# A two-layer MLP kernel: operand blocks of the second layer copied to PSUM ahead of the subtraction that makes their low half

## The chip, the core and the metric

One core of a Trainium2 chip runs the whole program. The metric is device time of one execution in microseconds; the kernel before has a median of 1340.35 us over 3 runs (1339.38 to 1341.3). The engines go by these names: TensorE (PE in the profile, with PEld for its weight loads), VectorE (DVE), ScalarE (ACT), GpSimd (POOL) and SyncE (SP), which issues the DMAs.

## What is computed

A layer of a trunk: a gated DeltaNet mixer with a residual, then a squared-ReLU MLP with a residual, each behind an RMS norm, and a final RMS norm. 1024 tokens, width 1024, 4096 hidden channels, all fp32. Cut to the part that matters here:

```python
def sq_relu_mlp(h, w1, w2):
    return jnp.square(jax.nn.relu(h @ w1)) @ w2

def reference(x, ...):
    h = x
    h = h + gated_deltanet(rmsnorm(h, norm_mix_g[0]), ...)
    h = h + sq_relu_mlp(rmsnorm(h, norm_mlp_g[0]), mlp_w1[0], mlp_w2[0])
    return rmsnorm(h, final_norm_g)
```

## The kernel before

The program has four stages, one after the other: the mixer (to about 554 us), its output projection and the second norm (to 642), the first MLP layer (to 973) and the second (973 to 1324), with the final norm woven into the end of the last.

**Split operands.** TensorE multiplies in the fp32r format. To keep fp32's accuracy each operand is split into a high part (the value rounded to fp32r) and a low part (the value less the high part, again as fp32r), and a product is three matmuls: high by high, high by low, low by high (L1284, L1285, L1286 in the second layer; L1285 is the one that needs the low part of the moving operand, L1286 that of the stationary one). `split` (L79) does this: with "act" ScalarE casts the source to the high part (L81), then VectorE subtracts the high part from the source (L86).

**The second layer** is the product of the squared hidden channels (A) and w2 (B). The 32 tiles of hidden channels are cut into five groups, numbered 0 to 4, of 2, 2, 4, 4 and 4 channel tiles in each half (`GROUPS`). In a group A and B are cut in two both ways, and the four blocks of the result come of seven products P1 to P7 (Winograd's form of Strassen's method), so the operands are the blocks A11, A12, A22, B11, B21, B22 and the block sums S1 to S4 (of A) and T1 to T4 (of B). The loop `for q, (n, k, p, x, y) in enumerate(seq)` runs over the 35 products: n is the group, k the place in the group, p the product's number, x and y its operands. The order of a group is P1, P2, P5, P7, P6, P4, P3; in the last group P1, P5, P7, P6, P4, P2, P3. A product has four blocks of 128 tokens (m), each in a PSUM bank of its own, from four banks in turn; for each m there are 2 or 4 steps of three matmuls 128x128 by 128x512, so a product is 24 matmuls in groups 0 and 1 and 48 in the others.

**Operands.** A block lies in SBUF in one or two units of 128x1024 fp32 (two channel tiles by 512 columns), the tiles `u`. They are loaded by DMA from w2 and from the spilled hidden channels (`hd`), or made by `make_sum` (L918), on GpSimd but for T1 and T3, which VectorE makes; a sum mostly takes the place of one of its operands. `make_operand` (L928) splits a block, unit by unit, into a slot of `hT` (two slots for either side): while product q runs, the operands of product q+1 go into the slots that product q-1 used, so the cast waits for TensorE to have read those. 7 x (2 + 2 + 4 + 4 + 4) = 112 units are split so.

**After each block m** the bank is added on VectorE (L1214) to the running sum of its product, in `oT` (P2, P3, P4, P7) or the tiles P1, P5, P6 (`extra`); in group 0 the sums in `extra` begin with a ScalarE copy (L1302). In the last group `finish_up` combines the seven sums (more adds L1214 on VectorE and GpSimd, with both operands in SBUF), then come the squares of the final norm on ScalarE (L1221), its roots on GpSimd (L1225, L76) and the rows of y on VectorE (L1239).

**What sets the order.** The code is written in program order with `next(pieces)` after each m, and a scheduler orders the instructions of each engine; each engine then runs its own queue strictly in order, waiting on semaphores. [...] 

Of the kernel before, what the change touches and what calls it, by code (L numbers as in the profile page):

```python
# [8 lines left out]
F32 = mybir.dt.float32  # L9
F32R = mybir.dt.float32r  # L10
AF = mybir.ActivationFunctionType
ALU = mybir.AluOpType

P = 128
T = 1024          # tokens
D = 1024          # model width
KT = D // P       # contraction tiles of the model width
NT = T // P       # token tiles, also chunks of the recurrence
H = 8             # heads
# [3 lines left out]
NW = 8            # buffers of half a weight tile, split  # L23
NRAW = 2          # buffers of half a weight tile, as loaded
NKK = 12          # key-side buffers
# [3 lines left out]
def trunk_kernel(  # L29
# [18 lines left out]
    ps = ctx.enter_context(tc.tile_pool(name="ps", bufs=1, space=bass.MemoryType.PSUM))  # L48
    dram = ctx.enter_context(tc.tile_pool(name="dram", bufs=1, space=bass.MemoryType.DRAM))

    def ps_gemm(name):
        """Two banks, one for each half of the columns."""
        return [ps.tile([P, 512], F32, tag="gemm", name=f"{name}_{i}", bufs=4) for i in range(2)]

    def ps_tp(name):
        return ps.tile([P, 512], F32, tag="tp", name=name, bufs=2)

    # ---------------------------------------------------------------- constants
# [6 lines left out]
    pvec = const.tile([P, 105], F32, tag="pvec", name="pvec")       # conv taps, g_o, g_mix  # L65
# [6 lines left out]
    def rsqrt_pool(dst, src, n, add=EPS):  # L72
        """dst = (src + add) ** -0.5 on [P, n]."""
# [4 lines left out]
    # -------------------------------------------------- weights, split exactly  # L78
# [14 lines left out]
    def load_split(hi, lo, src, name, eng):  # L93
        """Load half a weight tile and split it."""
        split(hi, lo, load_raw(hi, src, name), eng)

    def load_wtile(w, c0, name, eng):
        """Columns c0..c0+127 of w as [k, kt, 128], in two halves of kt; eng: None for the loads alone."""
# [10 lines left out]
    def load_wrow(src, name, eng, pool, tags):  # L109
        """128 rows of w as [k, D]."""  # L110
# [6 lines left out]
    def gemm_T(pt, w, act, half, during=None):  # L117
        """pt[half] = w_tile^T @ act for half the tokens, act given as [k, 2, kt, T]; during: what to emit before which step."""
# [10 lines left out]
    def norm_to_T(src, t, g_bc, dstT, pool, hs, name):  # L129
        """RMS norm of token tile src [P, D], times g, transposed into dstT [k, 2, kt, T]."""  # L130
# [23 lines left out]
    # ------------------------------------------------------ norm, gates, decays  # L154
# [3 lines left out]
    def small(shape, parts=P):  # L158
        """Room for a small array."""
# [8 lines left out]
    # per-channel vectors, from rows to columns  # L168
# [19 lines left out]
    tpv = ps.tile([P, 512], F32, tag="ch", name="tpv", bufs=2)  # L188
    nc.tensor.transpose(tpv[:, 0:105], pv, ident[0:105, 0:105])
    # taps and g_o are halved: silu(x) = (tanh(x / 2) + 1) * x / 2  # L190
    # (g_o is negated, as the heads' outputs are)
# [5 lines left out]
    def norm_x(t, sq, sc):  # L197
        """Token tile t over its root mean square."""
# [14 lines left out]
    def turn_x(g, tags):  # L213
        """Four token tiles, times g_mix, into xT."""
        tps = [ps.tile([P, 512], F32, tag=tag, name=f"tpx_{g}_{kt}", bufs=4 if tag == "gemm" else 2)
# [23 lines left out]
    # the small projections: high and low parts of the weights side by side  # L239
# [7 lines left out]
    def decays():  # L247
        tab = ps.tile([P, 512], F32, tag="ch", name="tab", bufs=2)
# [9 lines left out]
        # softplus(t) = max(t, 0) + log1p(e), e = exp(-|t|);  # L258
        # log1p(e) = ln(u) + (e - (u - 1)) / u, u = 1 + e rounded
# [14 lines left out]
        # g = -exp(a_log) * softplus(a + dt_bias), as [token, head, tile]  # L274
# [3 lines left out]
        # cumulative sums within a chunk, counted from the middle of the chunk  # L278
# [11 lines left out]
        pg = ps.tile([P, 512], F32, tag="ch", name="pg", bufs=2)  # L290
# [5 lines left out]
        # ne = -exp(G), G from the start of the chunk  # L296
# [1047 lines left out]
```

## Time and profile before

| | |
|---|---|
| median of 3 runs | 1340.35 us |
| span of the profiled execution, first to last instruction | 1335.6 us |
| what lies around the span, median less span | 4.75 us |
| PE busy | 1267.3 us, 95% |
| DVE busy | 1013.7 us, 76% |
| ACT busy | 619.1 us, 46% |
| POOL busy | 410.9 us, 31% |
| second layer, first to last matmul | 972.95 to 1323.95 us |
| the costliest group of instructions: L86 of `hT` on DVE | 204.6 us |

The profile is of one execution; its own time is the span and what lies around it, and the profile gives the span alone. A busy share is an average over the four stages. Matmuls are pipelined, so a busy TensorE isn't TensorE at its full pace: the pace is read from the number of matmuls in a stretch, and the granted clock is given beside it.

### The profile page before, as it was taken

The page shows a single profiled execution, that of the slowest core. Times are in us where ns is not written, and L with a number is a line of the kernel's source. Part 1 is how long each engine was busy: PE and PEld are TensorE (multiplying, and loading weights), DVE is VectorE, ACT ScalarE, POOL GpSimd, SP SyncE. Part 2 cuts the span into 40 slices and gives each one's busy share as a digit, 9 for nine tenths or more (in the row PEclk, how much of TensorE's full clock was granted, in tenths as well). Part 3 has the DMA queues.
Part 4 walks back from the last instruction along what each step waited for, and adds up shares of the span by engine and source line. Part 5 has one row for each costly group of instructions (what it writes and reads, how often), then busy time and mean ns, then how long its engine had stood idle before and what let it go on. Part 6 is the DMA issues. An engine that isn't in the chain of part 4 may idle for free.

```text
span 1335.6 us, 18642 instructions
## 1 busy us (share of the span) xinstructions
PE 1267.3 (95%) x6668; PEld 1034.4 (77%) x6668; DVE 1013.7 (76%) x1745; ACT 619.1 (46%) x1458; POOL 410.9 (31%) x339
## 2 busy tenths in 40 slices
PE   7999999999999999999969999999999899899986
PEld 5788888888888887788747888888876678687765
DVE  6799599589759867544796555555579988989998
ACT  4671655554654466333345554555554323333223
POOL 6220122211121112101463233323143615354565
PEclk9999999999999999999979999999999989999988
DMA  5242212122221212311313333333152134142003
GB/s 177 81 108 60 55 49 67 50 60 56 61 75 38 67 40 77 113 48 48 134 47 103 113 109 110 111 115 107 48 220 95 63 100 152 36 138 79 0 1 126
DMA packets 101871, 111.48 MB, mean 83 GB/s; under 512 B 23401, under 2 KB 73746, under 8 KB 101778
## 3 DMA queue, kind: packets, MB, share of 16 engines
q1 hardware_dynamic: 101778, 110.28, 27.0%
q8 instruction: 53, 0.87, 0.3%
q14 instruction: 40, 0.33, 0.1%
HBM read 89.26 MB, written 21.00 MB: 83 GB/s over the span
## 4 chain that ended last, share of the span: by engine, by line
PE 76%; DVE 13%; issue 5%; POOL 3%; ACT 2%; DMA 1%; POOLq 0%; DVEq 0%; ACTq 0%; SPq 0%
PE p L1066 7%; PE p L1065 7%; PE p L1064 7%; DVE hT L86 6%; PE p L1285 5%; PE p L1286 4%; PE p L1284 4%; PE pv L127 2%; PE pv L125 2%; PE pv L126 2%; PE pq L127 2%; PE pq L125 2%; PE pq L126 2%; PE pg L127 2%; PE pg L126 2%
## 5 line engine op out<-in xcount | busy, mean ns | idle before, releaser
L86 DVE TENSOR_TENSOR hT<-u,hT 128x1024 fp32r<-128x1024 f32 x112 | 204.6, 1845 | 20.4 <-ACT hT L81 20.3
L81 ACT CAST hT<-u 128x1024 fp32r<-128x1024 f32 x112 | 111.3, 1049 | 210.6 <-PE p L1285 144.0
L1285 PE MATMUL p<-hT 128*128 128x512 f32 x448 | 180.6, 403 | 22.1 <-DVE hT L86 21.7
L918 POOL TENSOR_TENSOR u<-u,u 128x1024 f32<-128x1024 f32 x48 | 139.1, 2904 | 170.4 <-DVE hT L86 124.8
L1284 PE MATMUL p<-hT 128*128 128x512 f32 x448 | 178.7, 399 | 7.2 <-DVE oT L1214 6.0
L1286 PE MATMUL p<-hT 128*128 128x512 f32 x448 | 178.2, 398 | 0.0
L76 POOL TENSOR_TENSOR sso<-sso,cons 128x1 f32<-128x1 f32 x64 | 42.0, 657 | 266.2 <-DVE sso L611 266.1
L1285 PEld LDWEIGHTS p<-hT 128*128 128x128 f32 x448 | 86.5, 193 | 45.8 <-DVE hT L86 28.2
L1284 PEld LDWEIGHTS p<-hT 128*128 128x128 f32 x448 | 86.4, 193 | 29.8 <-DVE oT L1214 5.6
L1286 PEld LDWEIGHTS p<-hT 128*128 128x128 f32 x448 | 86.7, 194 | 17.8
L1088 DVE TENSOR_TENSOR u<-u,p 128x512 f32<-128x512 f32 x56 | 38.4, 685 | 42.1 <-PE p L1066 42.1
L125 PE MATMUL pg<-xT,wh_g 128*128 128x512 f32 x128 | 54.4, 425 | 0.0
L125 PE MATMUL pq<-xT,wh_q 128*128 128x512 f32 x128 | 53.9, 421 | 0.0
L1214 DVE TENSOR_TENSOR oT<-oT,p 128x512 f32<-128x512 f32 x80 | 52.8, 675 | 1.5 <-PE p L1286 1.5
L125 PE MATMUL pv<-xT,wh_v 128*128 128x512 f32 x128 | 53.6, 419 | 0.0
L125 PE MATMUL pk<-xT,wh_k 128*128 128x512 f32 x128 | 53.1, 414 | 0.0
L127 PE MATMUL pg<-xT,wl_g 128*128 128x512 f32 x128 | 52.4, 409 | 0.0
L1064 PE MATMUL p<-T,wh_S 128*128 128x512 f32 x120 | 48.1, 401 | 4.4 <-ACT T L81 3.5
L127 PE MATMUL pv<-xT,wl_v 128*128 128x512 f32 x128 | 51.7, 404 | 0.0
L126 PE MATMUL pg<-xT,wh_g 128*128 128x512 f32 x128 | 51.7, 404 | 0.0
L126 PE MATMUL pv<-xT,wh_v 128*128 128x512 f32 x128 | 51.5, 402 | 0.0
L126 PE MATMUL pk<-xT,wh_k 128*128 128x512 f32 x128 | 51.1, 399 | 0.0
(312 smaller groups left out, 3470.0 us busy)
## 6 DMA issues: line engine op xcount, KB each, us to landing
u<-in_mlp_w_dram SPq DMA_DIRECT2D x34, 512.0 KB, 3.5
ra<-in_mlp_w_dram SPq DMA_DIRECT2D x28, 512.0 KB, 4.3
u<-hd SPq DMA_DIRECT2D x28, 512.0 KB, 5.7
hd<-u SPq DMA_DIRECT2D x24, 256.0 KB, 3.3
xt<-in_x_dram SPq DMA_DIRECT2D x8, 512.0 KB, 5.2
wr_k<-in_gdn_w_in_dram SPq DMA_DIRECT2D x16, 256.0 KB, 3.2
wr_q<-in_gdn_w_in_dram SPq DMA_DIRECT2D x16, 256.0 KB, 3.0
wr_v<-in_gdn_w_in_dram SPq DMA_DIRECT2D x16, 256.0 KB, 2.9
```

The costliest lines, as they stand in the source:

```text
L81: nc.scalar.copy(h_ap, src)
L86: (nc.gpsimd if low == "pool" else nc.vector).tensor_tensor(out=l_ap, in0=src, in1=h_ap.bitcast(F32), op=SUB)
L125: nc.tensor.matmul(o, hi, act[:, 0, kt, s], start=(kt == 0), stop=False)
L126: nc.tensor.matmul(o, hi, act[:, 1, kt, s], start=False, stop=False)
L127: nc.tensor.matmul(o, lo, act[:, 0, kt, s], start=False, stop=(kt == KT - 1))
L918: (V if name in ("T1", "T3") else G).tensor_tensor(out=o, in0=a, in1=b, op=op)
L1064: nc.tensor.matmul(o, hi[:, kt, :], act(0, kt), start=(j == 0 and kt == 0), stop=False)
L1065: nc.tensor.matmul(o, hi[:, kt, :], act(1, kt), start=False, stop=False)
L1066: nc.tensor.matmul(o, lo[:, kt, :], act(0, kt), start=False, stop=(j == n - 1 and kt == 3))
L1284: nc.tensor.matmul(o, hid(0, kt)[:, s], w(0, kt), start=(kt == 0), stop=False)
L1285: nc.tensor.matmul(o, hid(0, kt)[:, s], w(1, kt), start=False, stop=False)
L1286: nc.tensor.matmul(o, hid(1, kt)[:, s], w(0, kt), start=False, stop=(kt == g - 1))
```

## The change

In the second layer `make_operand` no longer calls `split`. ScalarE casts a unit to the high part as before, and copies the unit as it is into two PSUM banks (`cp`); VectorE subtracts the high part from that copy, so its first operand lies in PSUM instead of SBUF. There are two such buffers of two banks each, in the banks of `tp` and `ch`, which the mixer has left by then; to that end these two go into a pool of their own, closed after the mixer. The squares of the final norm write their discarded output into one of the `cp` buffers. The rest of the program is as it was; the diff also takes out comments and docstrings, which shifts the line numbers. In the changed kernel the cast is L944, the copy L945, the subtraction L946, the block sums L923, the adds L1226, the squares L1233 and the rows of y L1251.

```diff
+    psx = tc.tile_pool(name="psx", bufs=1, space=bass.MemoryType.PSUM)
+    px = psx.__enter__()
...
     def ps_tp(name):
-        return ps.tile([P, 512], F32, tag="tp", name=name, bufs=2)
+        return px.tile([P, 512], F32, tag="tp", name=name, bufs=2)
...
     gdn.__exit__(None, None, None)
+    psx.__exit__(None, None, None)
+    psc = tc.tile_pool(name="psc", bufs=1, space=bass.MemoryType.PSUM)
+    pc = psc.__enter__()
...
         for u, t in enumerate(us):
             hi, lo = (hT[:, hl, 4 * side + 2 * u : 4 * side + 2 * u + 2, HALF[s]] for hl in range(2))
-            split(hi, lo, t, "act")
+            cp = two_banks(f"cp{n}_{name}_{u}")
+            nc.scalar.copy(hi, t)
+            nc.scalar.copy(cp, t)
+            V.tensor_tensor(out=lo, in0=cp, in1=hi.bitcast(F32), op=SUB)
             if u == len(us) - 1:
...
+    def two_banks(name):
+        return pc.tile([P, 2, 512], F32, tag="cp", name=name, bufs=2)
...
-        nc.scalar.activation(ps_tp(f"sq{t}_{n}"), oT[:, t, HALF[n]], AF.Square, scale=1.0 / 32, accum_out=sss[t][:, n : n + 1])
+        nc.scalar.activation(two_banks(f"sq{t}_{n}")[:, 0, :], oT[:, t, HALF[n]], AF.Square, scale=1.0 / 32, accum_out=sss[t][:, n : n + 1])
```

The scheduler sets the new instructions into the queues. In the lines below a name such as `cp3_S1_0` is the copy of unit 0 of operand S1 in group 3, `u18` a unit in SBUF, `p2_0_2_1` the bank of group 0, product P2, block m = 1, and the last number of a name counts tiles.

ScalarE's queue in group 3 before, the casts of S1 and T1 (two units each) and the first of the next operands:

```order
L81 CAST hT_5905<-u18_9220 128x2x512
L81 CAST hT_5905<-u9_9211 128x2x512
L81 CAST hT_5905<-u19_9221 128x2x512
L81 CAST hT_5905<-u0_6640 128x2x512
L81 CAST hT_5905<-u2_6642 128x2x512
```

and now:

```order
L945 COPY cp3_S1_0_10479<-u18_9231 128x1024
L945 COPY cp3_S1_1_10497<-u19_9232 128x1024
L944 CAST hT_5908<-u18_9231 128x2x512
L944 CAST hT_5908<-u9_9222 128x2x512
L944 CAST hT_5908<-u19_9232 128x2x512
L945 COPY cp3_T1_0_10515<-u9_9222 128x1024
L944 CAST hT_5908<-u0_6647 128x2x512
L945 COPY cp3_T1_1_10533<-u0_6647 128x1024
L945 COPY cp3_S3_0_10557<-u2_6649 128x1024
```

The copies of S1's two units come ahead of its casts, those of T1's among the casts.

VectorE's queue at the start of the second layer before: the low parts of B21 and A12 (the second product's operands), the sums T1 and T3, and the first adds of P2 with the low parts of S1 and T1 beside them:

```order
L86 TENSOR_TENSOR hT_5905<-u6_6646,hT_5905 128x2x512
L1088 TENSOR_TENSOR u2_15_9110<-u2_15_9110,p1_15_3_9190 128x512
L86 TENSOR_TENSOR hT_5905<-u1_6641,hT_5905 128x2x512
L918 TENSOR_TENSOR u17_9219<-u5_6645,u4_6644 128x1024
L918 TENSOR_TENSOR u5_6645<-u7_6647,u5_6645 128x1024
L86 TENSOR_TENSOR hT_5905<-u16_9218,hT_5905 128x2x512
L1214 TENSOR_TENSOR oT_84<-oT_84,p2_0_2_0_9277 128x512
L86 TENSOR_TENSOR hT_5905<-u17_9219,hT_5905 128x2x512
```

and now:

```order
L1100 TENSOR_TENSOR u2_15_9117<-u2_15_9117,p1_15_3_9201 128x512
L946 TENSOR_TENSOR hT_5908<-cp0_A12_0_9257,hT_5908 128x2x512
L923 TENSOR_TENSOR u17_9230<-u5_6652,u4_6651 128x1024
L946 TENSOR_TENSOR hT_5908<-cp0_B21_0_9269,hT_5908 128x2x512
L923 TENSOR_TENSOR u5_6652<-u7_6654,u5_6652 128x1024
L1226 TENSOR_TENSOR oT_87<-oT_87,p2_0_2_0_9292 128x512
L946 TENSOR_TENSOR hT_5908<-cp0_S1_0_9299,hT_5908 128x2x512
L1226 TENSOR_TENSOR oT_87<-oT_87,p2_0_2_1_9304 128x512
L946 TENSOR_TENSOR hT_5908<-cp0_T1_0_9311,hT_5908 128x2x512
```

The order of A12 and B21 has changed, and the sum T1 (L923 of u17) stands between them.

ScalarE's queue at the end of the last group before, the last casts (S4 and B22 of the last product) and the squares of the final norm:

```order
L81 CAST hT_5905<-u11_9213 128x2x512
L81 CAST hT_5905<-u6_6646 128x2x512
L81 CAST hT_5905<-u7_6647 128x2x512
L81 CAST hT_5905<-u1_6641 128x2x512
L1221 ACTIVATE sq0_0_11119,ssf0_11118<-oT_84 128x512
L1221 ACTIVATE sq4_0_11122,ssf4_11121<-oT_84 128x512
L1221 ACTIVATE sq4_1_11124,ssf4_11121<-oT_84 128x512
L1221 ACTIVATE sq1_0_11146,ssf1_11145<-oT_84 128x512
L1221 ACTIVATE sq5_0_11149,ssf5_11148<-oT_84 128x512
L1221 ACTIVATE sq5_1_11151,ssf5_11148<-oT_84 128x512
```

and now:

```order
L944 CAST hT_5908<-u6_6653 128x2x512
L944 CAST hT_5908<-u7_6654 128x2x512
L944 CAST hT_5908<-u1_6648 128x2x512
L1233 ACTIVATE sq0_0_11344,ssf0_11343<-oT_87 128x512
L1233 ACTIVATE sq4_0_11347,ssf4_11346<-oT_87 128x512
L1233 ACTIVATE sq4_1_11349,ssf4_11346<-oT_87 128x512
L945 COPY cp4_S4_1_11366<-u7_6654 128x1024
L1233 ACTIVATE sq1_0_11373,ssf1_11372<-oT_87 128x512
L1233 ACTIVATE sq5_0_11376,ssf5_11375<-oT_87 128x512
L1233 ACTIVATE sq5_1_11378,ssf5_11375<-oT_87 128x512
L945 COPY cp4_B22_0_11395<-u6_6653 128x1024
L1233 ACTIVATE sq2_0_11402,ssf2_11401<-oT_87 128x512
```

Three of the four copies of the last product stand between the squares. On VectorE the matching piece, from the add of P2's second block on, is now:

```order
L1226 TENSOR_TENSOR oT_87<-oT_87,p2_4_2_1_11353 128x512
L946 TENSOR_TENSOR hT_5908<-cp4_S4_1_11366,hT_5908 128x2x512
L1226 TENSOR_TENSOR oT_87<-oT_87,p2_4_2_2_11382 128x512
L1251 SCALAR_TENSOR_TENSOR y4_0_11411<-oT_87,ssf4_11346,gx3_0_9236 128x512
L946 TENSOR_TENSOR hT_5908<-cp4_B22_0_11395,hT_5908 128x2x512
L1251 SCALAR_TENSOR_TENSOR y4_1_11414<-oT_87,ssf4_11346,gx3_1_9237 128x512
L1226 TENSOR_TENSOR oT_87<-oT_87,p2_4_2_3_11417 128x512
L1251 SCALAR_TENSOR_TENSOR y5_0_11446<-oT_87,ssf5_11375,gx3_0_9236 128x512
L946 TENSOR_TENSOR hT_5908<-cp4_B22_1_11430,hT_5908 128x2x512
L1251 SCALAR_TENSOR_TENSOR y5_1_11449<-oT_87,ssf5_11375,gx3_1_9237 128x512
```

where before the four low parts of the last product stood ahead of the second add and of all rows of y.

## Rows read from the trace of the kernel before

**Rows 1.** Busy time of each engine by stage: five groups, a clear stretch, the end

```profile
core 0: us, PE busy (x) PEld busy (x) DVE busy (x) ACT busy (x) POOL busy (x), PEclk, DMA share, GB/s
972.95:1018.14 45.19, 41.55 (x169) 31.98 (x168) 41.63 (x33) 23.32 (x31) 23.32 (x9) 0.96 0.57 209
1018.14:1067.70 49.56, 41.74 (x168) 32.24 (x169) 47.85 (x46) 17.72 (x18) 25.16 (x10) 0.97 0.19 64
1067.70:1151.01 83.31, 79.25 (x336) 64.86 (x337) 72.40 (x62) 24.94 (x27) 33.73 (x12) 0.96 0.31 101
1151.01:1232.93 81.92, 77.05 (x337) 62.83 (x336) 73.02 (x61) 27.36 (x29) 36.12 (x13) 1.00 0.32 103
1232.93:1323.95 91.02, 82.08 (x337) 65.48 (x335) 89.72 (x79) 31.19 (x51) 54.16 (x34) 0.94 0.05 19
1083.72:1138.12 54.40, 54.40 (x241) 45.05 (x240) 46.59 (x38) 19.66 (x21) 26.64 (x10) 1.00 0.41 136
1323.95:1335.60 11.65, 0.14 (x1) 0.00 (x0) 7.30 (x10) 2.17 (x5) 6.05 (x7) 0.69 0.58 218
```

**Rows 2.** Who waited for whom: total us, times, longest us

```profile
PE p L1285 <- DVE hT L86: 21.7, 12, 2.4
...
POOL u L918 <- DVE hT L86: 124.8, 26, 17.1
```

**Rows 3.** TensorE's timeline after one wait: start, us, instruction, [idle before]

```profile
1021.05 0.79 PE L1285 MATMUL p<-hT 128*128 128x512 f32 x1 [2.43 <-DVE hT L86]
...
1022.06 0.63 PE L1284 MATMUL p<-hT 128*128 128x512 f32 x1
1022.49 0.63 PE L1285 MATMUL p<-hT 128*128 128x512 f32 x1
```

**Rows 4.** VectorE's subtractions and adds: ns least/median/most; then busy us, mean ns

```profile
L86 DVE TENSOR_TENSOR hT<-u,hT x112: 1208/1225/3412, 956.6 to 1313.0; 128x1024 fp32r<-128x1024 f32 x112
...
L145 DVE TENSOR_TENSOR hT<-tpn_h,hT x16: 678/680/692, 572.0 to 648.9; 128x512 fp32r<-128x512 f32 x16
...
L1214 DVE TENSOR_TENSOR oT<-oT,p x80: 671/674/687, 983.9 to 1328.2; 128x512 f32<-128x512 f32 x80
...
L1214 DVE TENSOR_TENSOR oT<-oT,P x12: 677/922/2510, 1267.5 to 1308.4; 128x512 f32<-128x512 f32 x12
...
L86 DVE TENSOR_TENSOR hT<-u,hT 128x1024 fp32r<-128x1024 f32 x112 | 204.6, 1845 | 20.4 <-ACT hT L81 20.3
```

**Rows 5.** Block sums: GpSimd's durations; then VectorE's and GpSimd's timeline in group 2

```profile
L918 POOL TENSOR_TENSOR u<-u,u x48: 2354/3258/3392, 976.2 to 1275.5; 128x1024 f32<-128x1024 f32 x48
...
1138.62 3.43 DVE L918 TENSOR_TENSOR u<-u,u 128x1024 f32<-128x1024 f32 x1
1141.97 0.67 DVE L1214 TENSOR_TENSOR oT<-oT,p 128x512 f32<-128x512 f32 x1
1142.57 1.21 DVE L918 TENSOR_TENSOR u<-u,u 128x1024 f32<-128x1024 f32 x1
1143.71 0.67 DVE L1214 TENSOR_TENSOR oT<-oT,p 128x512 f32<-128x512 f32 x1
...
1135.22 5.75 POOL L918 TENSOR_TENSOR u<-u,u 128x1024 f32<-128x1024 f32 x2 [1.16 <-DVE hT L86]
```

**Rows 6.** ScalarE's casts and squares: ns least/median/most; then its timeline

```profile
L81 ACT CAST hT<-u x112: 1037/1048/1071, 955.5 to 1303.4; 128x1024 fp32r<-128x1024 f32 x112
L81 ACT CAST wh_A<-ra x42: 603/624/624, 698.1 to 959.3; 128x512 fp32r<-128x512 f32 x42
...
L1221 ACT ACTIVATE sq<-oT x16: 579/580/604, 1311.9 to 1328.9; 128x512 f32<-128x512 f32 x16
...
1149.62 3.89 ACT L81 CAST hT<-u 128x1024 fp32r<-128x1024 f32 x4 [8.99 <-PE p L1285]
```

**Rows 7.** The start of the second layer: timelines of VectorE and GpSimd

```profile
976.07 4.57 DVE L918 TENSOR_TENSOR u<-u,u 128x1024 f32<-128x1024 f32 x2 [0.23 <-ACT u L1084]
...
976.17 10.04 POOL L918 TENSOR_TENSOR u<-u,u 128x1024 f32<-128x1024 f32 x3 [22.05 <-ACT u L1084]
```

More of the change, by code (lines that the diff above doesn't have):

```diff
@@ L187, in trunk_kernel @@
     nc.sync.dma_start(nea, a_log.partition_broadcast(P))
-    tpv = ps.tile([P, 512], F32, tag="ch", name="tpv", bufs=2)
+    tpv = px.tile([P, 512], F32, tag="ch", name="tpv", bufs=2)
     nc.tensor.transpose(tpv[:, 0:105], pv, ident[0:105, 0:105])
@@ L213, in turn_x @@
     def turn_x(g, tags):
-        tps = [ps.tile([P, 512], F32, tag=tag, name=f"tpx_{g}_{kt}", bufs=4 if tag == "gemm" else 2)
+        tps = [(ps if tag == "gemm" else px).tile([P, 512], F32, tag=tag, name=f"tpx_{g}_{kt}", bufs=4 if tag == "gemm" else 2)
                for kt, tag in enumerate(tags)]
@@ L247, in decays @@
     def decays():
-        tab = ps.tile([P, 512], F32, tag="ch", name="tab", bufs=2)
+        tab = px.tile([P, 512], F32, tag="ch", name="tab", bufs=2)
         for t in range(NT):
@@ L289, in decays @@
         nc.vector.memset(hi[64:128, :], 1.0)
-        pg = ps.tile([P, 512], F32, tag="ch", name="pg", bufs=2)
+        pg = px.tile([P, 512], F32, tag="ch", name="pg", bufs=2)
         gv = gg.rearrange("p h t -> p (h t)")
@@ L308, in decays @@
         nc.scalar.activation(cd, cd, AF.Exp)
-        tg = ps.tile([P, 512], F32, tag="ch", name="tg", bufs=2)
+        tg = px.tile([P, 512], F32, tag="ch", name="tg", bufs=2)
         nc.tensor.transpose(tg[0:64, 0:P], gs[:, 0], ident)
@@ L567, in scan @@
         for c in range(NT):
-            ch = ps.tile([P, 4, P], F32, tag="ch", name=f"ch{h}_{c}", bufs=2)
+            ch = px.tile([P, 4, P], F32, tag="ch", name=f"ch{h}_{c}", bufs=2)
             po = ch[:, 3, :]
@@ L1314, in trunk_kernel @@
     hold.__exit__(None, None, None)
+    psc.__exit__(None, None, None)
 _INS = [
```

## Prediction

> **What bounds the kernel now.** I read the busy times by stage first, then what TensorE waits for, then how long one instruction takes alone and in company. The change touches only the second layer, which runs from 973 to 1324 us of the 1335.6 us span, so the share of busy time over the whole kernel says little. In the one stretch of it without a wait, TensorE does five products of 48 matmuls in 54.40 us [rows 1], that is 10.88 us for a product, and half of it, 5.44 us, in groups 0 and 1, whose products have 24 matmuls. Seven products are then 38.1 us in groups 0 and 1 and 76.2 us in groups 2, 3 and 4. The five stages take 45.2, 49.6, 83.3, 81.9 and 91.0 us [rows 1], so they lose 7.1, 11.5, 7.1, 5.8 and 14.8 us, together **46.3 us**. That is all that a change in this layer can give while the matmuls stay the same, apart from the 11.65 us after the last matmul [rows 1]. Of the 46.3, some 29.3 us are idle TensorE (stage less busy time, summed) and some 12 us are half clock: the granted clock of the five stages is 0.96, 0.97, 0.96, 1.00 and 0.94, and stage times (1 - clock) sums to 12.1 [rows 1]. The rest is lost in gaps of a matmul or two.
>
> Who makes TensorE wait? In the second layer it is above all VectorE's subtraction, L86: 21.7 us in 12 waits [rows 2]. [...]
>
> Why is VectorE late? The subtraction of 128x1024 takes 1.225 us as a rule, but its longest is 3.412 us and its mean 1.845 us [rows 4]. What stretches it stands beside it: GpSimd's block sums L918, which take 2.354 us at best, 3.258 us in the middle [rows 5]. Two VectorE sums of the same form show it within 4 us: 3.43 us at 1138.62, beside a GpSimd pair that runs 1135.22 to 1140.97, and 1.21 us at 1142.57, when GpSimd is idle [rows 5]. VectorE's adds with one operand in PSUM don't show it: 80 of them lie between 671 and 687 ns, in the same stages, while the form with both operands in SBUF spreads from 677 to 2510 ns [rows 4]. Summed over the stages VectorE is busy 325 of 351 us, and 89.7 of 91.0 in group 4, ScalarE 125 us [rows 1].
>
> **The change part by part.** *The subtraction from PSUM.* The nearest row is L145, the same subtraction with its first operand in PSUM and fp32r output, at half the size: 680 ns, against 671 to 687 for the adds [rows 4]. An SBUF form goes from 0.677 us at 512 columns to 1.225 at 1024 [rows 4], so I take 1.22 us for 1024 out of PSUM, with bounds of 1.21 (the shortest now) and 1.36 (twice 680 ns). 112 times (1.845 - 1.22) is **70 us less VectorE**. From start to start such an instruction takes 0.07 us less than its duration, 1.14 us, and an add 0.60 [rows 5].
>
> [...] The rows show no difference between the two sources at 512 columns. [...]
>
> *The copy on ScalarE.* Before, no ScalarE copy from SBUF to PSUM of 1024 columns stands in the trace. The cast, SBUF to SBUF, takes 1.048 us at 1024 columns and four in a row take 3.89 us, 0.97 apiece; an activation of 512 columns into PSUM takes 0.58 us [rows 6]. Bounds: 1.0 (0.58 and 0.42 for 512 columns more, which is what lies between the cast's 0.624 and 1.048 [rows 6]) and 1.16 (twice 0.58). I take 1.0 us, 112 us more ScalarE, 125 + 112 = 237 of 351. In a product of 10.88 us that is four casts and four copies, 7.9 us; in group 1 3.9 of 5.44 us; in group 0 three of seven products have four copies of sums into P too, L1302, some 0.5 us each by the 512-column row, 2.0 us more, so 5.9 of 5.44 there, but 33 of 38.1 us over the group. It fits, but barely in group 0.
>
> *Where the copy stands in the queue.* In the steady products the order sets the first two copies ahead of the casts, which wait for TensorE to leave the slot; before, ScalarE stood idle there, 8.99 us ahead of one set of four casts [rows 6]. From the slot's release, about 1.4 us before a product begins, ScalarE then has four casts and two copies, 5.9 us, and VectorE 1.2 us: all is there some 6 us into a product of 10.88. Four to five us of slack, with subtractions that no longer grow to 3.4 us. I cost it at nothing in groups 2 and 3; the slack is its cover.
>
> *Two buffers for the copies.* A third copy waits for the subtraction of the first. In the steady order a cast lies between, and the subtraction (1.2) fits beside two casts (1.9): nothing.
>
> *The operand is free earlier.* L918 overwrites operand blocks and waits 125 us for L86 in all [rows 2]; it will wait for ScalarE's cast and copy instead, and runs nearer to its 2.35 us. GpSimd is busy 23 to 54 us of a stage [rows 1], so that costs and gives nothing by itself. SP's loads into freed blocks go out earlier too, some in another order; the DMA share of the last four stages is 0.05 to 0.32 [rows 1], nothing.
>
> *The start of group 0.* Here the change adds a wait. The second product needs B21's low part. ScalarE's copy of it stands behind the last square of the first layer, for which GpSimd's S1 sum waits too, and that begins at 976.17 now [rows 7]; with the copy of A12 ahead of that square it ends near 977.6. VectorE, in order, does A12's subtraction (to 977.3) and the T1 sum ahead of B21's; the pair T1, T3 took 4.57 us beside GpSimd's sums [rows 7]. T1 alone, 1.2 to 2.9 us, will end at 978.5 to 980.2 and the subtraction 1.2 us later, whereas the second product begins at 978.4 (972.95 and 5.44) and wants it at its second matmul. A stall of 1 to 3 us, and half clock after it. Of its 7.1 us I leave group 0 with 5.5: a gain of 1.6.
>
> *Group 1.* VectorE has 14 subtractions (14 x 1.14 = 16.0), 28 adds at a pitch of 0.6 (16.8) and three SBUF sums at 1.2 to 3.4 (3.6 to 10): 36 to 43 of 38.1 us. It is still nearly the bound: I leave 3 of 11.5, a gain of 8.5.
>
> *Groups 2 and 3.* 28 x 1.14 + 28 x 0.6 and four SBUF sums (5 to 14) are 54 to 63 of 76.2 us. One us left of each: gains 6.1 and 4.8.
>
> *Group 4.* Its VectorE work has 16 SBUF adds more (677 ns to 2510, middle 922 [rows 4]), all in four products: with 16 subtractions and 16 adds, 18.2 + 9.6 + 14.8 = 42.6 of 43.5 us. Balanced. And in the last-but-one product the squares of L1221 now come ahead of the last three copies: B22's second copy stands behind nine squares, the last three of which wait for the third add, 8.2 + 0.7 us into the product; at 0.6 each they end 10.8 us in, the copy 11.8, and its subtraction, behind the fourth add and a row of y, 13.4 to 13.8 us in. The last product begins at 10.88 and wants it seven matmuls later, at 12.5: a stall of about 1 us. I leave 5 of 14.8: a gain of 9.8.
>
> *After the last matmul.* In the 11.65 us there VectorE is busy 7.30 [rows 1], with adds and rows of y that had queued; with less queued this may shrink by 1 or 2. Zero in the sum.
>
> The sum is 1.6 + 8.5 + 6.1 + 4.8 + 9.8 = **30.8 us**. Against the profile, 1335.6 becomes 1304.8; what lies around the span is 4.75 us to the median of 1340.35, so **1309.5 us**.
>
> **The rivals.** *ScalarE's line eats part of it.* If in the 14 products of 5.44 us and in group 4 each set of low parts comes one copy (1.0 us) late, with a half clock here and there, some 14 us go back: about 1324. For it speaks that 5.9 of 5.44 us stand in ScalarE's queue in three products, against it the idle time in rows 6. *All stalls go*, also at the start and in group 4: a gain of 40 to the whole 46.3, 1294 to 1300. For it speaks that only VectorE's 16 L918 and 16 late adds then have both operands in SBUF; the order at the start speaks against it. *The subtraction is stretched as before*, since it still reads its high part from SBUF and writes there: then VectorE stays at 1.845 us, and each of 12 waits is up to a copy longer, 1340 to 1352. The 80 adds of rows 4 read and write SBUF just so and were never stretched. *Slower: the copy into two banks is the bound.* The layer's ScalarE work without copies is 125 us; with 112 copies of c us it fills the 351 us of now at c = 2.0. If a two-bank copy took 2.1 us, it would be 360 us, 1350. The point is twice my 1.0, and rows 6 show 0.58 for half of it, so this needs a cost that no row hints at. *It doesn't do what it says*: the order shows each of the 112 copies and subtractions, so no chance is set aside.
>
> **How the numbers follow.** Forecast, 1300 to 1316 around 1309.5: 0.64. ScalarE eats part, 1316 to 1332: 0.19. All stalls go, 1294 to 1300: 0.08. Stretched as before: 0.05, of which 0.04 within 0.2% of the median (2.7 us, about what a measurement of this kernel can tell) and 0.01 slower. The copy as the bound, slower: 0.04. So faster 0.91, same 0.04, slower 0.05. The range is 1295 to 1327: it leaves out some 0.05 of the second case, 0.01 of the third and the last two, below 0.2 together.
>
> **What would show it.** L86's place: 112 subtractions from cp near 1.22 us with little spread, whatever GpSimd does; ScalarE's copies near 1.0 us; the wait of TensorE for the subtraction falling from 21.7 us to some 6, left at the second product of group 0 and the last of group 4; stages 2 and 3 near 77 us; granted clock 1.00 in groups 2 and 3. It is wrong if the subtractions spread as before, if copies take well over 1.0 us, or if TensorE's waits move to ScalarE's casts or copies.

## The result and the profile after

The changed kernel takes **1294.32 us** (median of 4 runs, 1293.30 to 1295.62) against 1339.87 for the kernel before (4 runs beside it, 1338.58 to 1341.30): a ratio of **0.966**, with a 95% interval of 0.965 to 0.968, or 45.5 us less. The forecast of 1309.5 had the direction and the place of the gain and was 15 us short of its size; the time lies 0.7 us below the low end of the range.

Here are the stages of the second layer after the change, the five groups and what follows the last matmul (stretch, its length, then the busy time of each engine, the granted clock, the DMA share and the GB/s):

```profile
core 0: us, PE busy (x) PEld busy (x) DVE busy (x) ACT busy (x) POOL busy (x), PEclk, DMA share, GB/s
972.19:1014.24 42.05, 40.65 (x169) 32.36 (x168) 31.33 (x31) 35.95 (x45) 23.77 (x9) 0.96 0.62 229
1014.24:1053.27 39.03, 38.45 (x168) 31.61 (x169) 36.53 (x46) 30.67 (x32) 21.16 (x10) 1.00 0.23 78
1053.27:1129.59 76.32, 76.32 (x338) 62.99 (x336) 64.28 (x66) 53.16 (x55) 32.05 (x13) 1.00 0.35 118
1129.59:1205.75 76.16, 76.16 (x338) 63.06 (x336) 59.45 (x61) 54.13 (x57) 31.27 (x12) 1.00 0.31 104
1205.75:1282.73 76.98, 76.47 (x337) 62.79 (x335) 68.97 (x81) 55.66 (x77) 48.75 (x35) 1.00 0.08 31
1282.73:1292.10 9.37, 0.15 (x1) 0.00 (x0) 5.00 (x7) 1.97 (x5) 3.90 (x5) 0.62 0.52 198
```

Read it beside [rows 1]. At the full pace the groups take 38.1, 38.1, 76.2, 76.2 and 76.2 us. They lost 7.1, 11.5, 7.1, 5.8 and 14.8 us before; they lose 4.0, 0.95, 0.15, 0 and 0.8 now, and the end shrank from 11.65 to 9.37. TensorE is the bound of this layer almost everywhere, with a granted clock of 1.00 in groups 1 to 4 and 0.96 in group 0. VectorE's work went from 324.6 us in the five groups to 260.6, ScalarE's from 124.5 to 229.6.

| stage | before | after | gain | gain forecast |
|---|---|---|---|---|
| group 0 | 45.19 | 42.05 | 3.1 | 1.6 |
| group 1 | 49.56 | 39.03 | 10.5 | 8.5 |
| group 2 | 83.31 | 76.32 | 7.0 | 6.1 |
| group 3 | 81.92 | 76.16 | 5.8 | 4.8 |
| group 4 | 91.02 | 76.98 | 14.0 | 9.8 |
| after the last matmul | 11.65 | 9.37 | 2.3 | 0 |
| ahead of the layer | 972.95 | 972.19 | 0.8 | 0 |
| span | 1335.6 | 1292.1 | 43.5 | 30.8 |

The durations of one instruction after the change (least/median/most in ns, then the times of the first and the last start): the subtraction L946 for two of the four kinds of block, ScalarE's copy into two PSUM banks L945, and the block sums L923 on both engines:

```profile
L946 DVE TENSOR_TENSOR hT<-cp_S,hT x32: 1208/1224/1226, 983.2 to 1267.7; 128x1024 fp32r<-128x1024 f32 x32
L946 DVE TENSOR_TENSOR hT<-cp_B,hT x24: 1207/1216/1225, 961.2 to 1273.8; 128x1024 fp32r<-128x1024 f32 x24
...
L945 ACT COPY cp_S<-u x32: 1000/1017/1044, 979.4 to 1266.6; 128x1024 f32<-128x1024 f32 x32
...
L923 POOL TENSOR_TENSOR u<-u,u x48: 2390/2422/3388, 975.8 to 1238.6; 128x1024 f32<-128x1024 f32 x48
L923 DVE TENSOR_TENSOR u<-u,u x16: 1215/1968/3420, 976.3 to 1200.5; 128x1024 f32<-128x1024 f32 x16
```

The longest subtraction takes 1.226 us, where it took up to 3.412 before [rows 4]. GpSimd's sums fell too, in the middle from 3.258 [rows 5] to 2.422 us: each engine had stretched the other. VectorE's own 16 sums, which still read both operands from SBUF, are stretched up to 3.42 us still, and more of them than before, when their middle was 1.216:

```profile
L918 DVE TENSOR_TENSOR u<-u,u x16: 1209/1216/3427, 976.1 to 1227.4; 128x1024 f32<-128x1024 f32 x16
```

What TensorE still waits for on VectorE's subtraction, in the whole layer (us in total, times, longest):

```profile
PE p L1297 <- DVE hT L946: 2.5, 3, 1.4
```

Before it was 21.7 us in 12 waits [rows 2]. The longest of the three is at the second product of group 0, as forecast.

### The profile page after: what moved, and what is told of

Same layout as the page of the kernel before. It is cut to its first block, busy times and chain, and to the rows that moved or that the text cites. A ratio compares the mean times of both kernels' runs of the same rounds, so it can differ in the third digit from the quotient of the medians.

```text
span 1292.1 us, 18789 instructions
## 1 busy us (share of the span) xinstructions
PE 1254.9 (97%) x6668; PEld 1031.8 (80%) x6668; DVE 946.5 (73%) x1745; ACT 725.7 (56%) x1570; POOL 390.8 (30%) x339
## 5 line engine op out<-in xcount | busy, mean ns | idle before, releaser
L1297 PE MATMUL p<-hT 128*128 128x512 f32 x448 | 175.6, 392 | 2.5 <-DVE hT L946 2.5
L1298 PE MATMUL p<-hT 128*128 128x512 f32 x448 | 175.1, 391 | 0.0
L1296 PE MATMUL p<-hT 128*128 128x512 f32 x448 | 174.1, 391 | 0.0
L923 POOL TENSOR_TENSOR u<-u,u 128x1024 f32<-128x1024 f32 x48 | 123.1, 2585 | 150.2 <-ACT cp_T L945 45.1
L944 ACT CAST hT<-u 128x1024 fp32r<-128x1024 f32 x112 | 112.6, 1050 | 30.7 <-PE p L1297 28.9
L1297 PEld LDWEIGHTS p<-hT 128*128 128x128 f32 x448 | 84.6, 189 | 21.7 <-DVE hT L946 3.8
L1296 PEld LDWEIGHTS p<-hT 128*128 128x128 f32 x448 | 84.2, 188 | 18.7 <-ACT P L1314 0.6
L1298 PEld LDWEIGHTS p<-hT 128*128 128x128 f32 x448 | 84.6, 189 | 17.2
L1226 DVE TENSOR_TENSOR oT<-oT,p 128x512 f32<-128x512 f32 x80 | 53.1, 678 | 12.9 <-PE p L1298 12.9
L127 PE MATMUL pg<-xT,wh_g 128*128 128x512 f32 x128 | 54.4, 425 | 0.0
L127 PE MATMUL pk<-xT,wh_k 128*128 128x512 f32 x128 | 53.1, 415 | 0.0
L1078 PE MATMUL p<-T,wl_S 128*128 128x512 f32 x120 | 48.3, 403 | 3.0 <-DVE wl_S L88 3.0
L946 DVE TENSOR_TENSOR hT<-cp_S,hT 128x1024 fp32r<-128x1024 f32 x32 | 39.1, 1222 | 16.5 <-ACT hT L944 14.1
```

What stands on the lines that cost most here:

```text
L127: nc.tensor.matmul(o, hi, act[:, 0, kt, s], start=(kt == 0), stop=False)
L923: (V if name in ("T1", "T3") else G).tensor_tensor(out=o, in0=a, in1=b, op=op)
L944: nc.scalar.copy(hi, t)
L946: V.tensor_tensor(out=lo, in0=cp, in1=hi.bitcast(F32), op=SUB)
L1078: nc.tensor.matmul(o, lo[:, kt, :], act(0, kt), start=False, stop=(j == n - 1 and kt == 3))
L1226: add = lambda eng, out, x: eng.tensor_tensor(out=out, in0=out, in1=x, op=ADD)
```

## The experiments

Two kernels of this section may start the second layer up to 5 us apart (972.2 to 977.0 us) although the first layer's code is the same; the same changed kernel, profiled twice, started it at 972.2 and at 974.3. So I compare the layer's stages, and totals only where they differ by more than that.

### The copy in SBUF instead of PSUM

My theory was that GpSimd's block sums stretch the subtraction as long as both its operands lie in SBUF. The rival was that the block is merely free earlier. This kernel keeps the copy and takes away PSUM alone:

```
-            cp = two_banks(f"cp{n}_{name}_{u}")
+            cp = (two_banks(f"cp{n}_{name}_{u}") if (n, name) in ((0, "A11"), (0, "B11")) else
+                  mp.tile([P, 2, 512], F32, tag="cps", name=f"cp{n}_{name}_{u}", bufs=2))
...
-    for p in (1, 5, 6):
+    for p in (1, 5):
         extra[p] = mp.tile([P, 4, 512], F32, tag=f"P{p}", name=f"P{p}")
+    extra[6] = extra[5]
```

> The changed kernel, but the copy goes to a buffer in SBUF instead of two PSUM banks; only A11 and B11 of group 0 keep their copies in PSUM. To make room the sums P5 and P6 share one tile, so that part of the output is not the reference's. All else stays: ScalarE's extra work, the earlier release of the operand block, the order. Theory A (GpSimd's sums stretch VectorE's subtraction as long as both its operands lie in SBUF, and the PSUM source ends that): the subtractions spread again from 1.2 to 3.4 us, mean 1.6 to 1.85, and the time goes back to 1325 to 1350 us. Theory B (the gain comes from the operand block being free earlier, or from another order on the engines): subtractions near 1.2 us or not, the time stays at 1290 to 1300 us.

Measured: **1351.33 us** (1349.39 to 1353.04), a ratio to before of 1.008 (1.006 to 1.010). The same subtraction, copy from SBUF, and GpSimd's sums:

```profile
L947 DVE TENSOR_TENSOR hT<-cp_S,hT x32: 1210/1226/3461, 989.5 to 1324.2; 128x1024 fp32r<-128x1024 f32 x32
L947 DVE TENSOR_TENSOR hT<-cp_T,hT x32: 1211/2240/3432, 994.9 to 1299.6; 128x1024 fp32r<-128x1024 f32 x32
...
L923 POOL TENSOR_TENSOR u<-u,u x48: 2380/3380/3407, 978.6 to 1283.3; 128x1024 f32<-128x1024 f32 x48
```

The stretch is back on both sides, and with it all of the loss and 12 us more. ScalarE's copies now wait for the stretched subtractions, 112.5 us in all against 41.4 in the changed kernel, which is the likely cause of the 12 us; no run takes it apart. The control, with the shared tile for two sums alone:

> The changed kernel with the one thing that the SBUF copy needed for room: P5 and P6 share one tile (that part of the output is not the reference's). Both theories: 1292 to 1297 us, the same as the changed kernel; if it is slower by more, the run with the copy in SBUF has to be read against this one.

It took 1299.35 us (1297.74 to 1300.34), 5 us above the changed kernel. Its profiled run is 6.5 us longer than that of the changed kernel, and 4.8 of these lie ahead of the layer, which starts at 976.97; the layer and its end differ by 1.6 us. Against this control the place of the copy is worth 52 us. The scheduler also orders the queues of the two a little differently (with the copy in SBUF, T1 stands ahead of A12's subtraction), which may be part of the 52 us.

### GpSimd's sums cut short, without the change and with it

```
-            (V if name in ("T1", "T3") else G).tensor_tensor(out=o, in0=a, in1=b, op=op)
+            if name in ("T1", "T3", "S1"):
+                (V if name in ("T1", "T3") else G).tensor_tensor(out=o, in0=a, in1=b, op=op)
+            else:
+                G.tensor_tensor(out=o[:, :, 0:16], in0=a[:, :, 0:16], in1=b[:, :, 0:16], op=op)
```

> The kernel before, with GpSimd's block sums cut to 16 of 512 columns in each half (all but S1; the other columns are left out), so that GpSimd hardly reads SBUF in the second layer, and VectorE still subtracts from SBUF. Theory A (contention with GpSimd's sums): the subtractions fall from a mean of 1.85 us to 1.2 to 1.3, the stalls go without the change, 1292 to 1302 us. Theory B (the gain comes from the earlier release or the order): the sums that no longer take 2.4 to 3.4 us give a little, 1325 to 1340 us.

> The changed kernel with the same cut of GpSimd's sums (most of their columns are left out). Theory A: what GpSimd does no longer matters much after the change; only VectorE's own sums with both operands in SBUF are still stretched, so 0 to 3 us less, 1290 to 1295 us. Theory B: the sums themselves are a bound, so it gives about as much as the same cut gave the kernel before.

Measured: the kernel **before** with this cut took **1298.26 us** (1296.97 to 1299.09), the changed kernel with it 1292.78 (1292.66 to 1292.85). The kernel before with the cut, its subtraction L86 and the sums that were cut, L921:

```profile
L86 DVE TENSOR_TENSOR hT<-u,hT x112: 1209/1219/3118, 959.7 to 1274.7; 128x1024 fp32r<-128x1024 f32 x112
...
L921 POOL TENSOR_TENSOR u<-u,u x40: 253/257/1185, 982.7 to 1238.2; 128x32 f32<-128x32 f32 x40
```

So 41 of the 45 us come without any copy, once GpSimd hardly reads SBUF; the same cut is worth 1.5 us after the change (3.7 us in the layer and its end). The cut alone would not exclude that sums done sooner are what helps, but the first experiment does: there the block is freed by ScalarE's cast and copy, as in the changed kernel, and ScalarE waits only 7.7 us for block sums (17.4 in the kernel before), yet the loss is back. Nor is another order of the queues the cause, for the kernel before with this cut has none of the new instructions and still gives 41 of the 45 us. The two together settle the cause: in these kernels GpSimd's sums and VectorE's subtractions hold each other up when both have two operands in SBUF, and one operand in PSUM ends it. With one input from PSUM the subtractions take 1.207 to 1.226 us in the changed kernel, and GpSimd's sums 2.422 us in the middle; with two from SBUF, when the copy lies there, the subtractions take up to 3.461 us and GpSimd's sums 3.380 in the middle.

### ScalarE's copy twice as dear

```
             nc.scalar.copy(cp, t)
+            nc.scalar.copy(cp, t)
```

> The changed kernel with each of the 112 copies into the two PSUM banks done twice, so that ScalarE pays about 2.0 us for each. It is the point from which the prediction let ScalarE become the bound. If my sum is right, the layer's ScalarE work is 230 + 112 = 342 us against a layer of 311: the time goes to some 1330 to 1355 us, with TensorE waiting for the casts and the subtractions. If ScalarE has more room than its busy time tells (work that can run ahead), less: 1310 to 1330.

Measured: 1341.30 us (1337.66 to 1343.27), ratio 1.0015 (1.0006 to 1.0025). The sum over its five groups and the 8.97 us behind them (the busy time of each engine, of 363.94 us):

```profile
sum 363.94, PE 326.23 PEld 254.94 DVE 264.13 ACT 332.63 POOL 158.77; mean PE 54.37 PEld 42.49 DVE 44.02 ACT 55.44 POOL 26.46
```

ScalarE is busy 333 of 364 us. The prediction let the copy eat the whole gain from 2.0 us each; two copies of 1.0 us eat it. The point was placed about rightly, though ScalarE still has 31 us free there, and the changed kernel is a factor of two away from it.

### One buffer for the copies instead of two

```
-        return pc.tile([P, 2, 512], F32, tag="cp", name=name, bufs=2)
+        return pc.tile([P, 2, 512], F32, tag="cp", name=name, bufs=1)
```

> The changed kernel with one buffer of two PSUM banks for the copies instead of two. Each copy then waits for the subtraction of the copy before it. My working costed two buffers at nothing in the steady order, because a cast of 1.05 us and the subtraction of 1.22 overlap: with one buffer the pair copy and subtraction becomes a chain of 2.3 us, 4 of them 9.2 us of a product's 10.88, 2 of them 4.6 of 5.44. Expected 1300 to 1325 us, the loss in groups 0, 1 and 4; if the slack were really 4 to 5 us in groups 2 and 3, these two stay near 76.3 us.

Measured: 1342.13 us (1340.58 to 1346.17), well above what I expected. Groups 2 and 3 take 85.3 and 84.9 us instead of 76.2. Timelines at the change to group 3 (start, us, engine and line, in brackets the idle time before it and what ended it), of VectorE, ScalarE and TensorE:

```profile
1139.61 3.41 DVE L923 TENSOR_TENSOR u<-u,u 128x1024 f32<-128x1024 f32 x1
1142.95 1.21 DVE L946 TENSOR_TENSOR hT<-cp_A,hT 128x1024 fp32r<-128x1024 f32 x1
```

```profile
1144.19 1.02 ACT L945 COPY cp_A<-u 128x1024 f32<-128x1024 f32 x1 [5.42 <-DVE hT L946]
...
1147.47 2.94 ACT L944 CAST hT<-u 128x1024 fp32r<-128x1024 f32 x3
```

```profile
1149.46 0.80 PE L1296 MATMUL p<-hT 128*128 128x512 f32 x1 [1.84 <-DVE oT L1226]
```

A subtraction that stands behind one of VectorE's stretched sums keeps the only buffer; ScalarE waits 5.42 us for it, and the copies and casts behind are late by as much. In the whole layer ScalarE waits 90.5 us for the subtractions (41.4 in the changed kernel) and VectorE 49.8 us for the copies (7.3). VectorE's adds, which free TensorE's banks, come late behind them, and here TensorE waits 1.84 us for one. My chain of 2.3 us for copy and subtraction left out that VectorE's other work lies in the chain. The prediction costed two buffers at nothing, which held; what I did not see is that the second buffer covers the whole gain. The 48 us are for the buffer together with the order that the scheduler makes for it: VectorE's queue is set quite differently with one buffer, and no run separates the two.

### The start: T1 behind B21, and S1 behind T1

The operands of the second product are split ahead of the sums, and T1 is issued behind B21's subtraction:

```
-            (V if name in ("T1", "T3") else G).tensor_tensor(out=o, in0=a, in1=b, op=op)
+            with tc.issue_after(lows[0, "B21"].ins) if (n, name) == (0, "T1") else nullcontext():
+                (V if name in ("T1", "T3") else G).tensor_tensor(out=o, in0=a, in1=b, op=op)
...
+    early = list(splits_for(1))
     sums_for(1)
```

> The changed kernel with the sum T1 of group 0 put behind the subtraction of B21 on VectorE. My theory of the start: the wait of 1.4 us for that subtraction and the half clock after it go, 2 to 3.5 us less, about 1291. Rival: the wait only moves to T1's users, products later, or the half clock has another cause, such as the end of the first layer: 1293 to 1295, no change that can be told.

Measured: 1295.49 us (1295.16 to 1296.29), no gain: group 0 takes 42.46 us. The wait has moved to the third product, as the rival had it (VectorE, then TensorE):

```profile
978.16 1.22 DVE L948 TENSOR_TENSOR hT<-cp_B,hT 128x1024 fp32r<-128x1024 f32 x1 [0.24 <-ACT cp_B L947]
979.31 4.89 DVE L924 TENSOR_TENSOR u<-u,u 128x1024 f32<-128x1024 f32 x2
984.12 0.67 DVE L1228 TENSOR_TENSOR oT<-oT,p 128x512 f32<-128x512 f32 x1
```

```profile
986.58 0.50 PE L1299 MATMUL p<-hT 128*128 128x512 f32 x1 [1.17 <-DVE oT L1228]
987.71 0.64 PE L1300 MATMUL p<-hT 128*128 128x512 f32 x1 [0.63 <-DVE hT L948]
```

VectorE's two sums take 4.89 us here, while GpSimd sums beside them (4.57 in the kernel before [rows 7]), and the adds behind them come late. So the next try leaves the order and takes the neighbour away: GpSimd's first sum waits for T1. The edit at the end of the layer was first tried by itself:

```
-                    if m:
+                    if m in (1, 3):
                         with tc.issue_after(summed_up.ins):
-                            final(m - 1)
+                            for t in {1: (0,), 3: (1, 2)}[m]:
+                                final(t)
```

> The changed kernel with the second row block of y computed behind the last add but one instead of ahead of it, so that VectorE's last add of P into the output comes sooner after the last matmul. Theory: the tail of 9.4 us shrinks by what VectorE spent on that row block there, 1 to 2 us: 1292 to 1293. Rival: the tail is set by the row blocks and their stores in all, whichever comes first: no change, or 1 us more.

Measured: 1294.94 us (1294.48 to 1295.19). From the end of the last matmul on, it went from 9.2 to 8.46 us, less than the theory's 1 to 2; in the total it can't be told from the scatter of the layer's start. Both edits together, the second being

```
-            late.extend((n, name) for name in names if name in SUMS)
+            late.extend((n, name) for name in (names[::-1] if q == 2 else names) if name in SUMS)
...
+                if name == "S1":
+                    tc.add_manual_dep(s.ins, first["T1"].ins.name, mybir.DependencyInfo(
+                        mybir.DependencyClass.Sync, mybir.DependencyReason.DATA), reason="T1 alone")
```

with the changed kernel beside them on the same chip:

> The changed kernel with both ends of the layer mended: GpSimd's first sum S1 of group 0 waits until VectorE's T1 is done, so that T1 runs alone (1.2 us instead of 3.0) and B21's subtraction behind it comes in time; and the second row block of y is computed behind the last add but one. My theory of the start: TensorE's wait of 1.4 us at the second product and the half clock after it go, group 0 from 42.0 to about 39.5 us; with 0.75 us off the tail 3 us less than the changed kernel on this chip. Rival: S1 comes 1.5 us later and the wait moves to the third product, as when T1 was put back: only the 0.75 us of the tail.

> The changed kernel as it is, on the same chip as the three beside it, to compare them with it: 1293 to 1296 us.

Measured: 1293.30 us (1292.95 to 1293.41; ratio to before 0.966, 0.965 to 0.968) against 1294.62 (1293.77 to 1295.80; 0.967, 0.966 to 0.969). The four runs of one lie below the four of the other, by 1.3 us in the median, less than half of the 3 us that I expected; from the first matmul of the layer to the end the two profiled runs differ by 2.2 us. T1 and its neighbours with both edits, on VectorE and GpSimd:

```profile
978.71 1.22 DVE L924 TENSOR_TENSOR u<-u,u 128x1024 f32<-128x1024 f32 x1
979.84 1.22 DVE L952 TENSOR_TENSOR hT<-cp_B,hT 128x1024 fp32r<-128x1024 f32 x1
```

```profile
980.14 10.61 POOL L924 TENSOR_TENSOR u<-u,u 128x1024 f32<-128x1024 f32 x4 [24.38 <-DVE u L924]
```

and in the changed kernel:

```profile
976.32 3.01 DVE L923 TENSOR_TENSOR u<-u,u 128x1024 f32<-128x1024 f32 x1
979.25 1.21 DVE L946 TENSOR_TENSOR hT<-cp_B,hT 128x1024 fp32r<-128x1024 f32 x1
```

T1 alone takes 1.22 us, beside GpSimd 3.01, and group 0 takes 39.49 us, as I wrote, with one wait of 0.62 us left at the third product. The changed kernel's own group 0 is 42.05 us in one profile and 40.97 in the other, so the edits at the start are worth 1.5 to 2.6 us. Of the versions that leave no work out it has the lowest median.

### Load or late pieces: VectorE as busy as before, in even pieces

The open question was why so little was left of the loss. The prediction left 3 us in group 1 and 5 in group 4 because VectorE would be nearly full there. This kernel makes VectorE as busy as it was before (323.5 us in the five groups against 324.6), without any long subtraction:

```
             V.tensor_tensor(out=lo, in0=cp, in1=hi.bitcast(F32), op=SUB)
+            V.tensor_tensor(out=lo[:, 0, :], in0=cp[:, 0, :], in1=hi[:, 0, :].bitcast(F32), op=SUB)
```

> The changed kernel with half of each subtraction done a second time, 0.6 us more for VectorE 112 times, so that VectorE is busy some 327 us of the layer, as long as before the change (325), but in instructions of even length. Theory V (VectorE's mean load sets the loss, as my prediction priced it: 3 us for 36 to 43 us of work in 38.1): groups 1 and 4 go over their pace and the time goes back to 1320 to 1340 us. Theory J (the loss comes from single subtractions of 3.4 us that arrive late, not from the load): 1297 to 1308 us.

Measured: 1332.90 us (1330.91 to 1334.53), within what the theory of the load said. Its five groups, columns as above:

```profile
974.06:1021.10 47.04, 42.03 (x170) 33.03 (x168) 38.82 (x45) 36.35 (x45) 23.20 (x9) 0.93 0.55 201
1021.10:1067.51 46.41, 41.19 (x169) 30.99 (x168) 43.02 (x59) 29.18 (x30) 21.38 (x9) 1.00 0.19 69
1067.51:1148.11 80.60, 77.99 (x337) 62.74 (x336) 77.23 (x96) 55.80 (x58) 29.46 (x13) 1.00 0.32 111
1148.11:1224.27 76.16, 76.16 (x337) 63.06 (x336) 72.82 (x88) 53.14 (x55) 30.43 (x12) 1.00 0.30 104
1224.27:1319.75 95.48, 83.37 (x337) 64.47 (x335) 91.63 (x108) 56.47 (x76) 44.52 (x35) 0.96 0.07 25
```

The total hides that the groups answer differently. Leave group 0 aside, where the start adds a loss of its own. Where VectorE's work exceeds the pace, the loss is the excess, which it must be at least, and 1 to 4 us more: 43.0 of 38.1 us in group 1 loses 8.3, 91.6 of 76.2 in group 4 loses 19.3 (before, 47.9 and 89.7 us lost 11.5 and 14.8 [rows 1]). Where it stays below, work in mostly even pieces loses nothing: group 3 with 72.8 of 76.2 us runs at the full pace. The kernel before had 73.0 us of VectorE work in that group [rows 1] and lost 5.8. There it was not the load but the moment: two subtractions stretched just as group 3 begins, and an add late behind a stretched sum at its last product. The kernel before, VectorE, GpSimd and TensorE at these places:

```profile
1150.04 6.15 DVE L86 TENSOR_TENSOR hT<-u,hT 128x1024 fp32r<-128x1024 f32 x2
...
1220.56 3.42 DVE L918 TENSOR_TENSOR u<-u,u 128x1024 f32<-128x1024 f32 x1
```

```profile
1148.47 6.65 POOL L918 TENSOR_TENSOR u<-u,u 128x1024 f32<-128x1024 f32 x2 [7.50 <-DVE hT L86]
```

```profile
1152.93 0.50 PE L1285 MATMUL p<-hT 128*128 128x512 f32 x1 [1.53 <-DVE hT L86]
...
1156.25 0.50 PE L1285 MATMUL p<-hT 128*128 128x512 f32 x1 [1.66 <-DVE hT L86]
...
1224.64 0.50 PE L1284 MATMUL p<-hT 128*128 128x512 f32 x1 [1.69 <-DVE oT L1214]
```

These three waits are 4.88 of the 5.8 us; with more even work TensorE has no wait in that group.

So each theory is half of it: in groups 1 and 4 the stretch made VectorE the bound, in group 3 it made single pieces late. In group 2, with 72.4 of 76.2 us [rows 1] and three waits of 5.9 us in all, it looks the same.

### The copy for one side alone

```
-            cp = two_banks(f"cp{n}_{name}_{u}")
+            cp = t if side else two_banks(f"cp{n}_{name}_{u}")
             nc.scalar.copy(hi, t)
-            nc.scalar.copy(cp, t)
+            if not side:
+                nc.scalar.copy(cp, t)
```

> The changed kernel with the copy into PSUM for one side of the products alone (the A and S blocks, 56 of 112); the B and T blocks are subtracted from SBUF as before. If the loss goes with the number of stretched subtractions, half of the 45 us comes back: 1312 to 1322 us. If VectorE has room enough for half of the stretch, as the small losses after the change suggest (0 to 1 us in groups 1 to 4), less than a third: 1295 to 1308 us.

Measured: 1311.58 us (1309.24 to 1314.05), ratio 0.981 (0.979 to 0.982): 17 of the 45 us come back, between my two ranges. It holds the comparison within one run: the subtractions from SBUF spread, those from PSUM beside them do not.

```profile
L947 DVE TENSOR_TENSOR hT<-u,hT x56: 1207/1226/3418, 963.0 to 1283.5; 128x1024 fp32r<-128x1024 f32 x56
L947 DVE TENSOR_TENSOR hT<-cp_S,hT x32: 1209/1216/1225, 983.7 to 1286.5; 128x1024 fp32r<-128x1024 f32 x32
```

Its groups 1 to 4:

```profile
1015.49:1056.72 41.23, 39.80 (x170) 31.14 (x168) 39.53 (x48) 23.72 (x24) 21.70 (x9) 1.00 0.23 77
1056.72:1137.36 80.64, 76.89 (x338) 62.77 (x336) 68.54 (x62) 38.96 (x41) 36.97 (x13) 1.00 0.31 105
1137.36:1216.38 79.02, 76.91 (x337) 62.92 (x337) 64.89 (x61) 40.86 (x43) 35.31 (x12) 1.00 0.32 107
1216.38:1298.72 82.34, 79.12 (x337) 63.86 (x336) 79.59 (x83) 43.41 (x65) 52.54 (x35) 0.98 0.09 32
```

The two kinds of loss show again: groups 1 and 4 exceed the pace a little (39.5 and 79.6 us) and lose 3.1 and 6.2; groups 2 and 3 lose 4.5 and 2.9 with 68.5 and 64.9 us of work.

## Why the prediction was right and where it was wrong

**Right: what bounds the layer and what ends it.** The subtraction of 1.22 us (measured 1.207 to 1.226), the copy of 1.0 us (medians 1.010 to 1.017), VectorE's 70 us less (64 in the five groups, where its own sums took 5.2 us more), ScalarE's 237 us (230), the granted clock of 1.00 in groups 2 and 3, and the stall of 1 to 3 us at group 0's second product: 1.38 us idle and then half the pace, 0.43 us from start to start at a granted clock of 0.50 (981.40 to 984.39 us). TensorE's timeline there:

```profile
980.51 0.50 PE L1297 MATMUL p<-hT 128*128 128x512 f32 x1 [1.38 <-DVE hT L946]
...
981.40 0.63 PE L1297 MATMUL p<-hT 128*128 128x512 f32 x1
981.83 0.63 PE L1298 MATMUL p<-hT 128*128 128x512 f32 x1
```

The half clock that the prediction put behind the stall is not shown to follow every one. It came after the wait of [rows 3] in the kernel before, with a granted clock of 0.50 from 1021.84 to 1024.00 us, and after the 1.38 us here; in the second profile of the changed kernel TensorE is idle for 1.39 us at the same product, and the granted clock of group 0 is 1.00.

The last product stalls once more, 0.52 us idle, where about 1 was forecast. The subtraction takes no longer from PSUM than from SBUF here: 112 subtractions from PSUM have medians of 1.215 to 1.224 us and a least of 1.207, those from SBUF had 1.225 and 1.208 [rows 4].

**Wrong: the term of what is left of the loss.** The step that failed is the loss that I left to the groups, 5.5, 3, 1, 1 and 5 us; in groups 1 and 4 it rested on a VectorE near its bound. The sum left 15.5 us of the 46.3; 5.9 were left. The forecast is 15.7 us above the profiled run of 1293.85 us, and these are the parts:

- *Group 4, 4.2 us.* The step was "42.6 of 43.5 us. Balanced", and then 5 us for it. Both were off. In the last four products VectorE does not do all 16 subtractions and all 16 SBUF adds: 4 and 6 of them run ahead, in earlier products, which the sum for four products alone did not allow; VectorE is busy 38.9 of 43.5 us there (row below), with 11 rows of y that I had not counted. And a VectorE that is full to 91% of the group's pace loses 0.8 us here, not 5.
- *Group 1, 2.0 us.* The working said 36 to 43 of 38.1 us and "nearly the bound"; 36.5 came, with one block sum in the stretch instead of three, and lost 0.95 us. Work just under the pace, in even pieces, cost next to nothing, as group 3 of the kernel with more VectorE work shows. I had no row for the 3 us; the clear stretch of [rows 1], 46.6 us of VectorE in 54.4 without a wait, was the nearest, and it spoke against it.
- *Groups 2, 3 and 0, 0.9, 1.0 and 1.5 us.* The 1 us in each of the first two had no cause named either. In group 0 the stall was sized rightly, and what I left beside it was too much.
- *The end, 2.3 us.* I named a gain of 1 or 2 and put zero in the sum.
- *Ahead of the layer, 0.8 us.* Scatter; the second profile of the changed kernel starts the layer 2.1 us later.
- *Around the span, 3.0 us.* I took median less span, 4.75 us. But every run lies 1.7 us above its own span (1293.85 and 1292.1, for one). The profiled execution of the kernel before was itself some 3 us faster than its median, so 4.75 mixed a constant with the scatter of single executions.

The last four products of the changed kernel:

```profile
1239.43:1282.89 43.46, 42.94 (x189) 34.88 (x187) 38.94 (x49) 31.40 (x52) 27.32 (x25) 1.00 0.15 56
```

**The rivals.** What came is the case to which I gave 0.08, that all stalls go: 40.5 of the 46.3 us within the groups. I held the order at the start against it, and that costs only the 1.4 us stall and, in one of the two profiles, the half clock behind it. The stretched subtraction is what the copy in SBUF brings back, 1351 us. ScalarE as the bound is reached with two copies, 1341 us, close to where it was put.

## What to carry to other kernels

When an instruction's spread reaches far above its median, look for what runs beside it on the other engine, and test it by shortening that neighbour: here 41 of 45 us came so, before any change was made. Price what an edit leaves by comparing each engine's work in a stage with the pace of the bound: here an excess cost itself and 1 to 4 us more, even work below it almost nothing, and only pieces late for a due time cost beyond that. Take the time around the span from a run and its own span, never from a median and another execution's span.

## What was unexpected of the hardware

- The stretch is mutual: with VectorE's subtractions out of the way GpSimd's sums fell from 3.26 to 2.42 us in the middle, and two of VectorE's sums beside them took 4.89 us, against 1.22 for one alone.
- A single ScalarE copy into two PSUM banks takes 1.00 to 1.04 us for 1024 columns, slightly less than the cast of the same block into SBUF (1.048 in the middle [rows 6]) or the same copy into SBUF (1.048 to 1.053 in the middle, in the kernel with the copy there).
- The second buffer of two PSUM banks, with the order that goes with it, is worth 48 us here, although in the changed kernel ScalarE is busy 74% of the five groups and VectorE 84%.
